# Splitting stored operands ahead of weight preparation, and a ninth early pair, in the two MLPs of a hybrid decoder trunk

## The chip, the core and the metric

The kernel runs on one core of one Trainium2 chip. The metric is device time in microseconds (us) of one execution of the whole program; the figure for a kernel is the median of its runs. All data is float32 in DRAM. The engines that matter are TensorE (PE: matmuls; PEld is its weight load), VectorE (DVE), ScalarE (ACT), GpSimd (POOL) and SyncE (SP); the last two are used here to start transfers (DMAs), each through a queue of its own.

## The reference, cut to what matters

The program computes one inference step of a two-layer decoder trunk, for a prompt of 1024 tokens and 8 single-token samples that share the weights:

```python
for l in range(DEPTH):                                    # DEPTH = 2
    h = rmsnorm(x, norm_mix[l]) * (1.0 + s1) + sh1
    out = even_mixer(h, ...) if l % 2 == 0 else mamba_mixer(h, ...)
    x = x + g1 * out
    h = rmsnorm(x, norm_mlp[l]) * (1.0 + s2) + sh2
    x = x + g2 * (jnp.square(jax.nn.relu(h @ mlp_w1[l])) @ mlp_w2[l])
```

The model width is 1024 and the inner width of the MLP 4096. The change lies in the MLP alone, that is in the last line, which is computed once in each layer. `h @ mlp_w1` is called the first projection here and the product with `mlp_w2` the second.

## The kernel before, in words

**Precision.** A float32 matmul is done as three matmuls of a reduced-precision type: each operand is split into a high part (a cast on ACT) and a low part (a subtraction on DVE), and `mm3` issues high x high (L501), high weight x low activation (L504) and low weight x high activation (L505).

**Seven products.** Each MLP projection is done by a Strassen-like scheme: instead of eight products of quarter matrices there are seven, of sums and differences of quarters, and their results are combined.

**First projections.** The 4096 inner columns are 16 pairs `p` of 2 x 128 columns. A pair has seven products `q` (1 to 7) of 24 matmuls of 128x258, so a layer has 112 products. The list `AOPS` says in which order TensorE runs them, `APREP` in which order their weights are prepared. Products 1 and 2 of a pair need only the plain input; the others need sums of input halves, which DVE and ACT make in the background (`mlp_sums`, `mlp_more_sums`) while the first products run. So the first LEAD pairs run their products 1 and 2 in front (`FRONT[0]`); they are called split pairs. A split pair's partial result (`U`) is parked in DRAM (`keep`, read back by `kept`), and its product 2 too (`B`). The last TAIL=4 pairs are split in the same way, at the end. `prep` makes the weights: a raw load on SP (`raw<-W`, 512 KB, two buffers), then, for products of sums, DVE additions (L411, L412, L420), the cast on ACT (`whi`, L441) and the subtraction on DVE (`wlo`, L442). Weights of products 1 and 2 of a split pair come from one raw load, with one cast (L435) and one subtraction (L436) of 1024 columns; the other products of a pair need both of its raw loads.

**Second projections.** 64 units run in seven stages `i`: units 0 to 47 have 48 matmuls of 128x258 each, eight units a stage, and units 48 to 63 have 24. A unit needs a weight (three buffers `whi`/`wlo`) and an operand `R[i,q]` of activations, four operands a stage, in two halves each. The operands lie in DRAM (`td`), are loaded through POOL by `load_op` (`rr<-td`, two transfers of 258 KB an operand) some units ahead, and are split by `split_op`, half by half: cast on ACT (L855), subtraction on DVE (L856). In stages 2 to 5 (the third to the sixth) a weight is a sum or a difference: a second load, `t<-W` or `t<-sd`, on SP, goes into one of four buffers `t6`, then DVE adds or subtracts (L461, L465 or L463) before the cast (L466) and the subtraction (L467). Plain weights have L476 and L477. In stages 2 and 3 the sums are stored to DRAM (`sd`) and read back in stages 3 and 5. When a unit pair is finished, its result leaves PSUM (four buffers `pd`) by DVE (L985, L992); TensorE can't start the next one before a buffer is free.

Each unit's Python code ran, in this order: matmuls and evictions, `prepare` (weights for three units ahead), `split_op`, `load_op`, and background steps (`ada_steps` adds four wide matmuls, L323, at every fourth unit of layer 0). A scheduler turns the program into one order for each engine, and an engine then runs its list strictly in that order, waiting at each instruction for what it needs. The order in which the code calls `prepare` and `split_op` sets where the two stand in the lists of ACT and DVE.

Of the kernel before, what the change touches and what calls it, by code (L numbers as in the profile page):

```python
# [33 lines left out]
AHEAD = 3  # L34
# [31 lines left out]
def odd_order():  # L66
# [5 lines left out]
    for i in range(8):  # L72
        if i == 3:
            o += z(3) + out(2) + [("dt", 0)] + bcx(4)
        else:
# [5 lines left out]

HX = TT // 2
NPAIR = NFF // 2
LEAD, TAIL = 8, 4
PROD = (1, 6, 7, 5, 2, 4, 3)

ENDS = range(LEAD), range(NPAIR - TAIL, NPAIR)
# [1 line left out]
FRONT = [[(p, q) for p in r for q in (1, 2)] for r in ENDS]  # L89
BACK = lambda r, qs=PROD: [(p, q) for p in r for q in qs if p not in SPLIT or q not in (1, 2)]  # L90
AREST = (BACK(range(2, NPAIR - TAIL)) + FRONT[1] + BACK(range(NPAIR - TAIL, NPAIR - 1))
         + BACK((NPAIR - 1,), (6, 7, 4, 5, 3)))
AOPS = FRONT[0] + BACK((0, 1), (6, 7)) + BACK((0, 1), (5, 4, 3)) + AREST

APREP = (FRONT[0] + BACK((0,), (6, 7, 4, 3)) + BACK((1,), (6, 7)) + BACK((0, 1), (5,)) + BACK((1,), (4, 3)) + AREST)
APOS = {o: i for i, o in enumerate(APREP)}


# [66 lines left out]
def kernel(ctx: ExitStack, tc: tile.TileContext, A: dict):  # L165
# [220 lines left out]
    wpos = [0]  # L386
# [36 lines left out]
    def prep(kind, idx, raw=None, into=None):  # L423
# [7 lines left out]
        if kind[0] == "a":  # L431
            l, ops = int(kind[1]), APREP[2 * idx:2 * idx + 2]
            if ops in ([(p, 1), (p, 2)] for p in SPLIT):
# [49 lines left out]
    def prepare(i):  # L483
        while len(units) <= min(i, limit[0] - 1):
            units.append(prep(*order[len(units)]))
# [310 lines left out]
    def mlp(l, gi, finish, more=None):  # L796
# [47 lines left out]
        def load_op(i, q):  # L844

            pool, tag = ((big, M["tags"][0]), (ph.pool, "hr"), (big, M["tags"][1]))[BSET[i][q // 2]]
            t = pool.tile([P, KT * 520], F32R, name="rr", tag=tag, bufs=2)
            hi, lo = R[i, q] = [t[:, j * 4 * HX:(j + 1) * 4 * HX].rearrange("p (k t) -> p k t", t=HX)
                                for j in range(2)]
            d = td[BOPND[BPROD[i]]][q // 2][:, q % 2 * 4:q % 2 * 4 + 4]  # L850

            def parts():
                for c in range(0, 4, 2):
                    src = lo[:, c:c + 2].bitcast(F32)
                    tc.keep_in_program_order(S.copy(hi[:, c:c + 2], src))  # L855
                    V.tensor_sub(lo[:, c:c + 2], src, hi[:, c:c + 2].bitcast(F32))  # L856
                    yield
            for c in range(0, 4, 2):
                dma_aux(lo[:, c:c + 2].bitcast(F32), d[:, c:c + 2])
            todo.append(parts())  # L860
# [15 lines left out]
        got = []  # L876
        for i, (p, q) in enumerate(AOPS):
            n = APOS[p, q]
            while len(got) <= n // 2:
                got.append(need(f"a{l}", len(got), AHEAD - 1))  # L880
            if i == 0:
                bg.drain(hgen.pop(3, None))
                sg = bg.add(mlp_sums())
                bg.step(sg)
            elif i == 2 * LEAD:
                bg.drain(hgen.pop(2), sg)
                sg = bg.add(mlp_more_sums())
            elif i == 2 * LEAD + 4:
                bg.drain(sg)
            if i == 2 * LEAD - 4:  # L890
                kept(0)
                kept(1)
            if q == 6:
                kept(p)
                if p and p + 1 in keep:
                    kept(p + 1)
            if p in SPLIT and q == (5 if p < 2 else 6) and p != NPAIR - TAIL:
                dma_aux(slot(p, 1), B[p])
            elif (p, q) == (NPAIR - 1, 1):
                kept(NPAIR - TAIL)  # L900
                kept(NPAIR - TAIL + 1)
                dma_aux(slot(NPAIR - TAIL, 1), B[NPAIR - TAIL])
            w = 512 * (n % 2), got[n // 2]
            pt = pd()
            product(w, q, pt)
            pv = pt[:, :, 0:HX // 2]
            if q == 1:
                U[p, 1] = t2(HX)
                S.copy(v2(U[p, 1]), pv)
                if p in SPLIT:  # L910
                    keep[p] = dr.tile([P, HX], F32, name="kept", tag=f"kept{p}")
                    dma_aux(keep[p], U[p, 1])
            elif q == 6:
                U[p, 1], U[p, 2] = saved.pop(p, U[p, 1]), t2(HX)
                V.tensor_sub(v2(U[p, 2]), v2(U[p, 1]), pv)
            elif q == 7:
                U[p, 3] = t2(HX)
                V.tensor_add(v2(U[p, 3]), pv, v2(U[p, 2]))
            elif q == 5:
                c = t2(HX)  # L920
                V.tensor_add(v2(c), pv, v2(U[p, 3]))
                V.tensor_add(v2(U[p, 2]), pv, v2(U[p, 2]))
                ff_out(p, q, c, -1.0)
            elif q == 2:
                c = t2(HX) if p in SPLIT else U[p, 1]
                V.tensor_add(v2(c), pv, v2(U[p, 1]))
                ff_out(p, q, c, 1.0)
            elif q == 4:
                c = U[p, 3] if p < NPAIR - 1 else t2(HX)
                V.tensor_add(v2(c), pv, v2(U[p, 3]))  # L930
                ff_out(p, q, c, -1.0)
            else:
                V.tensor_add(v2(U[p, 2]), pv, v2(U[p, 2]))
                ff_out(p, q, U[p, 2], 1.0)
            if n % 2:
                prepare(wpos[0] - 1 + AHEAD)
            if (p, q) == FRONT[1][-1]:
                load_op(0, 0)
                load_op(0, 1)
            elif p == NPAIR - 2 and q in (7, 5, 4, 3):  # L940
                split_op()
            if (p, q) == (NPAIR - 1, 5):
                split_op(4)
                load_op(0, 2)
                load_op(0, 3)
            bg.tick(2)
# [11 lines left out]
        for n, (i, hb, q, mp) in enumerate(BOPS):  # L958
            j = n % 8
            hi, lo = need(f"b{l}", n, AHEAD - 1)  # L960
            if n == 0 and more:
                ada[0] = more()
            elif i == 6 and hb == 0 and j == 0:
                ada_steps(99)
            elif n % 4 == 0:
                ada_steps(1)
            rh, rl = R[i, q]
            seq = BSEQ if i else BFIRST
            qs = [qq for qq, mm in seq if mm == mp]
            for m in (2 * mp, 2 * mp + 1):  # L970
                if q == qs[0]:
                    pts[m] = pd()
                pt = pts[m]
                for b in range(2) if hb is None else (hb,):
                    c = slice(b * hw, b * hw + hw)
                    mm3(pt[:, b, 0:hw], [(hi[:, o:o + P], lo[:, o:o + P], rh[:, k, c], rl[:, k, c])
                                         for k, o in ((k, 256 * k + m % 2 * P) for k in range(4))],
                        q == qs[0], q == qs[-1])
                if q == qs[-1]:
                    for o, th in BOUT[BPROD[i]]:  # L980
                        mt = 4 * o + m
                        gate = mod[:, gi + mt, 0:1]
                        if hb is None:
                            xv = v2(x[:, mt, th * HX:th * HX + HX])
                            V.scalar_tensor_tensor(xv, pt[:, :, 0:hw], gate, xv, op0=ALU.mult, op1=ALU.add)  # L985
                        else:
                            xv = x[:, mt, th * HX + hb * hw:th * HX + hb * hw + hw]
                            V.scalar_tensor_tensor(xv, pt[:, hb, 0:hw], gate, xv, op0=ALU.mult, op1=ALU.add)
                        if hb != 1:
                            sv = pt[:, 0, 0:4] if th else pt[:, 1, hw - 4:hw]  # L990
                            av = acc[:, mt, 4 * th:4 * th + 4]
                            V.tensor_add(av, sv, av)  # L992
            prepare(wpos[0] - 1 + AHEAD)

            split_op(((0, 2, 1, 1, 1, 1, 1, 1), (2, 2, 1, 1, 1, 1, 0, 2), (1, 1, 0, 0, 0, 0, 0, 0))[2 if i == 6 else i][j]
                     if i in (0, 1, 6) else (1, 1, 1, 1, 1, 1, 0, 2)[j])
            at = (4, 5, 6, 7) if i else (2, 3, 6, 7)
            if j in at and i < 6 and i + 1 + at.index(j) // 2 < 7:
                load_op(i + 1 + at.index(j) // 2, (2, 3, 0, 1)[at.index(j)])

            if i == 6 and j == 7 and hb == 0:
                V.tensor_mul(acc, acc, mod[:, gi:gi + KT, 1:9])
                for k in FOURS:
                    V.tensor_add(x[:, k, 512:520], acc[:, k], xs[:, k])
            if i >= 5:
                next(fin, None)
            bg.tick()
# [1147 lines left out]
```

## Time and profile before

| | |
|---|---|
| median of 3 runs | 2747.32 us (2745.33 to 2750.24) |
| the profiled execution | 2746.34 us; its span, first to last instruction, 2744.5 us |
| TensorE busy | 2643.4 us, 96% of the span |
| DVE, ACT, POOL busy | 1981.1 us (72%), 1484.1 us (54%), 266.2 us (10%) |
| mean granted TensorE clock | 0.985 of full speed |
| layer 0: first projections, second projections | 564 to 900 us, 900 to 1258 us |
| layer 1: first projections, second projections | 2058 to 2388 us, 2388 to 2733 us |

The profile gives busy time as a sum over the span; a share near 100% for TensorE says that most of what can be won is in the few places where it stands still. Those are found in the views of waits and of time lines, where each row has a start in us from the beginning of the span, a duration, the engine, the line, the operation, output and input, and in brackets how long the engine had been idle before and which instruction or transfer released it. A matmul of 128x258 has a duration of 0.28 us, but they overlap: starts are 0.12 us apart at full clock.

### The profile page before, as it was taken

The numbers are of one execution on the slowest core, as the hardware profiler recorded it, in microseconds if no ns is written. First come the engines' busy times: TensorE is split into PE (matmuls) and PEld (weight loads), VectorE is DVE, ScalarE is ACT, GpSimd is POOL, SyncE is SP. The second block draws the span as 40 slices with busy tenths as digits, with TensorE's granted clock in tenths as the row PEclk, the third lists the DMA queues.
The fourth block names the chain that finished last, engine by engine and source line by source line (L and its number), as shares of the span: only waits on it lengthen the run. The fifth ranks groups of instructions, "written<-read, shape, count | busy, mean of one in ns | idle before, by whom it ended". The sixth has DMA issues, their size and how long they took to land. (4 is left out here: it accounts for less than half of the span.)

```text
span 2744.5 us, 49358 instructions
## 1 busy us (share of the span) xinstructions
PE 2643.4 (96%) x19450; PEld 2436.2 (89%) x19450; DVE 1981.1 (72%) x3668; ACT 1484.1 (54%) x2411; POOL 266.2 (10%) x492
## 2 busy tenths in 40 slices
PE   6999999999999999899999999999999999999898
PEld 4888877889999999899899997787779999999897
DVE  5766542588867576676999988998778776766777
ACT  5785511174455332346887777878756445433234
POOL 0000000012313200000000000000001322310000
PEclk8999999999999999999999999999999999999999
DMA  8232356446648989744554535533335655879765
GB/s 307 66 100 84 97 190 206 139 153 198 228 155 261 387 296 353 255 142 128 161 159 156 185 125 158 146 129 108 120 115 163 228 186 188 290 282 368 269 216 162
DMA packets 191064, 525.63 MB, mean 192 GB/s; under 512 B 24432, under 2 KB 42544, under 8 KB 190832
## 3 DMA queue, kind: packets, MB, share of 16 engines
q1 hardware_dynamic: 142448, 355.25, 40.5%
q0 software_dynamic: 48384, 167.23, 16.6%
q8 instruction: 153, 2.51, 0.4%
q14 instruction: 79, 0.65, 0.1%
HBM read 408.59 MB, written 113.80 MB: 190 GB/s over the span
## 5 line engine op out<-in xcount | busy, mean ns | idle before, releaser
L501 PE MATMUL pg<-hh,whi 128*128 128x256 f32 (+2 forms) x1616 | 534.8, 331 | 7.5 <-ACT hh L603 5.9
L504 PE MATMUL pd<-rr,whi 128*128 128x258 f32 x1792 | 514.9, 287 | 17.2 <-DVE rr L856 17.1
L504 PE MATMUL pg<-hl,whi 128*128 128x256 f32 (+2 forms) x1616 | 522.0, 323 | 1.9 <-DVE hl L604 1.9
L505 PE MATMUL pg<-hh,wlo 128*128 128x256 f32 (+2 forms) x1616 | 521.3, 323 | 0.0
L501 PE MATMUL pd<-rr,whi 128*128 128x258 f32 x1792 | 511.3, 285 | 3.3 <-DVE racc L992 3.3
L505 PE MATMUL pd<-rr,wlo 128*128 128x258 f32 x1792 | 510.1, 285 | 3.6 <-DVE wlo L477 2.9
L476 ACT CAST whi<-raw 128x1024 fp32r<-128x1024 f32 x222 | 231.5, 1044 | 363.0 <-PE pg L504 217.4
L477 DVE TENSOR_TENSOR wlo<-raw,whi 128x1024 fp32r<-128x1024 f32 x222 | 270.8, 1221 | 204.5 <-ACT whi L476 196.9
L504 PEld LDWEIGHTS pd<-rr,whi 128*128 128x128 f32 x1792 | 343.4, 192 | 19.3 <-DVE rr L856 18.8
L501 PEld LDWEIGHTS pd<-rr,whi 128*128 128x128 f32 x1792 | 345.1, 193 | 10.7 <-issue 10.4
L501 PEld LDWEIGHTS pg<-hh,whi 128*128 128x128 f32 x1616 | 306.7, 190 | 50.2 <-issue 17.8
L505 PEld LDWEIGHTS pd<-rr,wlo 128*128 128x128 f32 x1792 | 343.9, 192 | 4.9 <-DVE wlo L477 3.7
L504 PEld LDWEIGHTS pg<-hl,whi 128*128 128x128 f32 x1616 | 306.9, 190 | 30.2 <-issue 4.8
L505 PEld LDWEIGHTS pg<-hh,wlo 128*128 128x128 f32 x1616 | 306.4, 190 | 24.1 <-issue 0.4
L501 PE MATMUL pd<-hh,whi 128*128 128x258 f32 x1024 | 291.8, 285 | 8.1 <-ACT hh L705 4.4
L504 PE MATMUL pd<-hh,whi 128*128 128x258 f32 x1024 | 290.6, 284 | 0.8 <-DVE hh L706 0.8
L505 PE MATMUL pd<-hh,wlo 128*128 128x258 f32 x1024 | 289.2, 283 | 0.0
L466 ACT CAST whi<-t 128x1024 fp32r<-128x1024 f32 x64 | 67.1, 1048 | 253.6 <-PE pd L504 166.6
L501 PEld LDWEIGHTS pd<-hh,whi 128*128 128x128 f32 x1024 | 194.6, 190 | 10.7 <-ACT hh L705 5.1
L504 PEld LDWEIGHTS pd<-hh,whi 128*128 128x128 f32 x1024 | 194.2, 190 | 1.9 <-DVE hh L706 1.4
L505 PEld LDWEIGHTS pd<-hh,wlo 128*128 128x128 f32 x1024 | 194.5, 190 | 0.0
L501 PE MATMUL pg<-ffh,whi 128*128 128x264 f32 (+2 forms) x544 | 177.3, 326 | 0.0
(338 smaller groups left out, 5815.1 us busy)
## 6 DMA issues: line engine op xcount, KB each, us to landing
raw<-W SPq DMA_DIRECT2D x375, 512.0 KB, 4.2
td<-x POOLq DMA_DIRECT2D x224, 258.0 KB, 4.0
rr<-td POOLq DMA_DIRECT2D x112, 516.0 KB, 7.2
t<-ada SPq DMA_DIRECT2D x192, 256.0 KB, 5.4
t<-W SPq DMA_DIRECT2D x32, 512.0 KB, 5.6
sd<-t SPq DMA_DIRECT2D x32, 512.0 KB, 6.2
t<-sd SPq DMA_DIRECT2D x32, 512.0 KB, 5.7
t<-csd SPq DMA_DIRECT2D x64, 256.0 KB, 4.5
```

Source lines behind the costliest of these rows:

```text
L466: S.copy(hi, h)
L476: S.copy(hi, raw)
L477: V.tensor_sub(lo, raw, hi.bitcast(F32))
L501: mm = PE.matmul(pt, wh, xh, start=first and i == 0, stop=False)
L504: PE.matmul(pt, wh, xl, start=False, stop=False)
L505: PE.matmul(pt, wl, xh, start=False, stop=last and i == n - 1)
```

## The change

It has two parts.

1. In the first projections LEAD goes from 8 to 9: pair 8 becomes a ninth split pair. Its products 1 and 2 do not stand behind those of pair 7 but between products 6 and 7 of pair 0 and products 6 and 7 of pair 1 (`AOPS`), and their weights are prepared behind those of pair 0 (`APREP`). The conditions on `i` that were multiples of LEAD are rewritten so that the first two still hold at positions 16 and 12; the third moves from 20 to 22, which in both lists is the start of product 5 of pair 0. In each layer there is one more raw load, and 258 KB more go to DRAM and back for each of `keep` and `B`.
2. In the second projections the call of `prepare` moves from ahead of `split_op` and `load_op` to behind them.

```diff
-LEAD, TAIL = 8, 4
+LEAD, TAIL = 9, 4
 PROD = (1, 6, 7, 5, 2, 4, 3)
...
-AOPS = FRONT[0] + BACK((0, 1), (6, 7)) + BACK((0, 1), (5, 4, 3)) + AREST
-
-APREP = (FRONT[0] + BACK((0,), (6, 7, 4, 3)) + BACK((1,), (6, 7)) + BACK((0, 1), (5,)) + BACK((1,), (4, 3)) + AREST)
+AOPS = FRONT[0][:-2] + BACK((0,), (6, 7)) + FRONT[0][-2:] + BACK((1,), (6, 7)) + BACK((0, 1), (5, 4, 3)) + AREST
+
+APREP = (FRONT[0][:-2] + BACK((0,), (6, 7, 4, 3)) + FRONT[0][-2:] + BACK((1,), (6, 7)) + BACK((0, 1), (5,))
+         + BACK((1,), (4, 3)) + AREST)
...
-            elif i == 2 * LEAD:
+            elif i == 2 * LEAD - 2:
                 bg.drain(hgen.pop(2), sg)
                 sg = bg.add(mlp_more_sums())
             elif i == 2 * LEAD + 4:
                 bg.drain(sg)
-            if i == 2 * LEAD - 4:
+            if i == 2 * LEAD - 6:
                 kept(0)
                 kept(1)
...
-            prepare(wpos[0] - 1 + AHEAD)
 
             split_op(((0, 2, 1, 1, 1, 1, 1, 1), (2, 2, 1, 1, 1, 1, 0, 2), (1, 1, 0, 0, 0, 0, 0, 0))[2 if i == 6 else i][j]
                      if i in (0, 1, 6) else (1, 1, 1, 1, 1, 1, 0, 2)[j])
             at = (4, 5, 6, 7) if i else (2, 3, 6, 7)
             if j in at and i < 6 and i + 1 + at.index(j) // 2 < 7:
                 load_op(i + 1 + at.index(j) // 2, (2, 3, 0, 1)[at.index(j)])
+            prepare(wpos[0] - 1 + AHEAD)
```

Lines of the changed kernel behind the lists are one higher than before (its L857 is L856 of before). Where the instructions stand now is seen best on DVE, at three places.

The first is layer 0's second projections, around unit 27. Before (the numbers behind names tell buffers apart: `rr_10635` is the third operand of stage 3 and `rr_10699` its fourth, which unit 27 uses; `t6_10902`, `t6_10963` and `t6_11024` carry the weight sums of units 27, 28 and 29):

```order
L467 TENSOR_TENSOR wlo_10821<-t6_10823,whi_10820 128x1024
L856 TENSOR_TENSOR rr_10635<-rr_10635 128x1032 x2
L465 TENSOR_TENSOR t6_10902<-t6_10902,raw_10904 128x1024
L465 TENSOR_TENSOR t6_10963<-t6_10963,raw_10965 128x1024
L467 TENSOR_TENSOR wlo_10900<-t6_10902,whi_10899 128x1024
L856 TENSOR_TENSOR rr_10699<-rr_10699 128x1032
L465 TENSOR_TENSOR t6_11024<-t6_11024,raw_11026 128x1024
L467 TENSOR_TENSOR wlo_10961<-t6_10963,whi_10960 128x1024
L856 TENSOR_TENSOR rr_10699<-rr_10699 128x1032
```

The same place in the changed kernel (`rr_10696` is the fourth operand; `t6_10912`, `t6_10973`, `t6_11034` are the sums of units 27, 28, 29):

```order
L468 TENSOR_TENSOR wlo_10836<-t6_10838,whi_10835 128x1024
L857 TENSOR_TENSOR rr_10696<-rr_10696 128x1032
L466 TENSOR_TENSOR t6_10912<-t6_10912,raw_10914 128x1024
L466 TENSOR_TENSOR t6_10973<-t6_10973,raw_10975 128x1024
L468 TENSOR_TENSOR wlo_10910<-t6_10912,whi_10909 128x1024
L857 TENSOR_TENSOR rr_10696<-rr_10696 128x1032
L466 TENSOR_TENSOR t6_11034<-t6_11034,raw_11036 128x1024
L468 TENSOR_TENSOR wlo_10971<-t6_10973,whi_10970 128x1024
```

The second half of unit 27's operand now stands ahead of the sum of unit 29 and the low part of unit 28, and the first half ahead of the sums of units 27 and 28.

The second place is layer 1's second projections, around unit 26. Before (`rr_27146` is the operand of unit 26; `t6_27402`, `t6_27463`, `t6_27524` are the sums of units 27, 28, 29; L985 evicts the results of units 22 and 23):

```order
L465 TENSOR_TENSOR t6_27402<-t6_27402,raw_27404 128x1024
L467 TENSOR_TENSOR wlo_27262<-t6_27264,whi_27261 128x1024
L465 TENSOR_TENSOR t6_27463<-t6_27463,raw_27465 128x1024
L985 SCALAR_TENSOR_TENSOR x_25826<-pd_27083,mod_84,x_25826 128x516
...
L985 SCALAR_TENSOR_TENSOR x_25827<-pd_27108,mod_84,x_25827 128x516
L992 TENSOR_TENSOR racc_25842<-pd_27108,racc_25842 128x4
L467 TENSOR_TENSOR wlo_27332<-t6_27334,whi_27331 128x1024
L856 TENSOR_TENSOR rr_27146<-rr_27146 128x1032 x2
```

The same place in the changed kernel (`rr_27151` is the operand of unit 26; `t6_27420` is the sum of unit 27 and `t6_27481` that of unit 28):

```order
L466 TENSOR_TENSOR t6_27420<-t6_27420,raw_27422 128x1024
L468 TENSOR_TENSOR wlo_27281<-t6_27283,whi_27280 128x1024
L857 TENSOR_TENSOR rr_27151<-rr_27151 128x1032
L986 SCALAR_TENSOR_TENSOR x_25842<-pd_27099,mod_84,x_25842 128x516
...
L857 TENSOR_TENSOR rr_27151<-rr_27151 128x1032
...
L468 TENSOR_TENSOR wlo_27355<-t6_27357,whi_27354 128x1024
L857 TENSOR_TENSOR rr_27215<-rr_27215 128x1032
L466 TENSOR_TENSOR t6_27481<-t6_27481,raw_27483 128x1024
```

Both halves of unit 26's operand and its weight's low part now stand ahead of the sum of unit 28.

The third place is layer 0's first projections, behind product 6 of pair 0. Before (`raw_5869` and `raw_5871` are the two raw loads of pair 1; L915 and L918 evict products 6 and 7 of pair 0):

```order
L915 TENSOR_TENSOR t2_5907<-t6_5737,pd_5882 128x516
L411 TENSOR_TENSOR t6_5873<-raw_5871 128x512
L420 TENSOR_TENSOR t6_5878<-raw_5869,raw_5871 128x512
L412 TENSOR_TENSOR t6_5873<-t6_5873,raw_5869 128x512
L706 TENSOR_TENSOR hr_5265<-x_83,hr_5264 128x2x516
L442 TENSOR_TENSOR wlo_5868<-t6_5873,whi_5867 128x512
```

The same place in the changed kernel (`raw_5869` is now the one raw load of pair 8 and `raw_5941` and `raw_5939` are those of pair 1):

```order
L916 TENSOR_TENSOR t2_5898<-t6_5737,pd_5873 128x516
L437 TENSOR_TENSOR wlo_5868<-raw_5869,whi_5867 128x1024
L707 TENSOR_TENSOR hr_5265<-x_83,hr_5264 128x2x516
L919 TENSOR_TENSOR t2_5935<-pd_5910,t2_5898 128x516
...
L412 TENSOR_TENSOR t6_5943<-raw_5941 128x512
L421 TENSOR_TENSOR t6_5948<-raw_5939,raw_5941 128x512
L413 TENSOR_TENSOR t6_5943<-t6_5943,raw_5939 128x512
```

The weights of pair 8, which need one load and no addition, stand where those of pair 1 stood, and those of pair 1 come two evictions later.

## Rows read from the trace of the kernel before

**Rows 1.** What TensorE waited for in the second projections: total us, times, longest; the first two rows are of 900 to 1258 us (layer 0), the last of 2388 to 2733 us (layer 1).

```profile
PE pd L504 <- DVE rr L856: 7.3, 3, 3.8
PE pd L501 <- DVE racc L992: 3.3, 1, 3.3
PE pd L504 <- DVE rr L856: 9.8, 4, 4.6
```

**Rows 2.** Busy time in stretches: us, PE (count of matmuls), PEld, DVE, ACT, POOL, granted clock, share of the DMA engines, GB/s. The first seven run from the last matmul at full clock before a wait to the first one at full clock behind it; two of the matmuls counted in each had started before the stretch. The last three are other stretches of the second projections, one of layer 0 and two of layer 1.

```profile
623.41:632.47 9.06, 4.50 (x22) 4.29 (x21) 7.15 (x12) 3.03 (x5) 0.54 (x1) 0.62 0.15 60
1063.39:1072.92 9.53, 6.55 (x32) 6.34 (x31) 7.31 (x8) 2.00 (x2) 0.00 (x0) 0.64 1.00 344
1117.80:1127.41 9.61, 5.79 (x28) 5.59 (x27) 5.64 (x5) 1.41 (x2) 0.00 (x0) 0.64 0.38 127
1156.76:1164.93 8.17, 4.86 (x28) 4.68 (x27) 7.54 (x13) 4.12 (x6) 0.00 (x0) 0.79 0.63 231
2110.61:2117.33 6.72, 5.04 (x27) 4.63 (x26) 6.63 (x12) 3.34 (x6) 1.08 (x2) 0.75 0.47 121
2538.16:2547.44 9.28, 4.64 (x23) 4.43 (x22) 9.28 (x14) 2.00 (x2) 0.00 (x0) 0.63 0.65 233
2599.79:2608.81 9.02, 4.77 (x27) 4.57 (x26) 4.82 (x5) 1.42 (x2) 0.00 (x0) 0.81 0.51 175
...
1000.00:1100.00 100.00, 97.02 (x778) 92.91 (x778) 67.24 (x82) 30.27 (x31) 8.26 (x16) 0.97 0.96 354
...
2480.00:2580.00 100.00, 95.22 (x774) 94.61 (x772) 71.57 (x92) 32.41 (x33) 8.42 (x17) 0.97 0.91 340
...
2515.00:2530.00 15.00, 15.00 (x127) 15.00 (x126) 6.06 (x6) 5.91 (x6) 3.16 (x6) 1.00 1.01 410
```

**Rows 3.** The time line of DVE before unit 27 of layer 0.

```profile
1061.10 1.23 DVE L856 TENSOR_TENSOR rr<-rr 128x1032 fp32r<-128x1032 f32 x1
1063.10 1.23 DVE L465 TENSOR_TENSOR t<-t,raw 128x1024 f32<-128x1024 f32 x1 [0.78 <-issue]
1064.24 1.22 DVE L467 TENSOR_TENSOR wlo<-t,whi 128x1024 fp32r<-128x1024 f32 x1
1065.38 1.23 DVE L856 TENSOR_TENSOR rr<-rr 128x1032 fp32r<-128x1032 f32 x1
```

**Rows 4.** The two loads of that operand, in the view of one tile from 1033 to 1036 us: the issues, and the time from issue to landing.

```profile
L230 POOL DMA_DIRECT2D rr<-td x2: 528/528/528, 1033.1 to 1033.7; - x2
...
DMA to landing us min/median/max: 7.0/8.3/9.6
```

**Rows 5.** The time line of DVE before unit 26 of layer 1.

```profile
2530.13 1.22 DVE L465 TENSOR_TENSOR t<-t,raw 128x1024 f32<-128x1024 f32 x1 [3.96 <-DMA raw<-W]
...
2536.60 1.23 DVE L465 TENSOR_TENSOR t<-t,raw 128x1024 f32<-128x1024 f32 x1 [4.11 <-DMA raw<-W]
...
2541.80 2.37 DVE L856 TENSOR_TENSOR rr<-rr 128x1032 fp32r<-128x1032 f32 x2
```

**Rows 6.** The time line of DVE before unit 35, in layer 0 and in layer 1.

```profile
1118.35 1.23 DVE L465 TENSOR_TENSOR t<-t,raw 128x1024 f32<-128x1024 f32 x1 [3.62 <-DMA t<-W]
...
1120.62 1.23 DVE L856 TENSOR_TENSOR rr<-rr 128x1032 fp32r<-128x1032 f32 x1
...
2600.78 1.23 DVE L465 TENSOR_TENSOR t<-t,raw 128x1024 f32<-128x1024 f32 x1 [2.20 <-DMA t<-W]
...
2603.05 1.23 DVE L856 TENSOR_TENSOR rr<-rr 128x1032 fp32r<-128x1032 f32 x1
```

**Rows 7.** Layer 0, units 40 and 41: two issues on SP's queue, then DVE.

```profile
1138.74 0.33 SPq L224 DMA_DIRECT2D t<-sd  x1
...
1148.59 0.33 SPq L224 DMA_DIRECT2D t<-sd  x1
...
1146.20 1.22 DVE L463 TENSOR_TENSOR t<-raw,t 128x1024 f32<-128x1024 f32 x1 [5.01 <-DMA t<-sd]
...
1156.39 1.22 DVE L463 TENSOR_TENSOR t<-raw,t 128x1024 f32<-128x1024 f32 x1 [6.69 <-DMA t<-sd]
1157.53 1.22 DVE L467 TENSOR_TENSOR wlo<-t,whi 128x1024 fp32r<-128x1024 f32 x1
1158.67 0.75 DVE L985 SCALAR_TENSOR_TENSOR x<-pd,mod,x 128x516 f32<-128x516 f32 x1
```

**Rows 8.** Layer 0, the first operand of stage 1: the cast of its first half on ACT and the weight cast behind it, the time from issue to landing of its two loads (issued from 926.5 us), and the first matmul of unit 7.

```profile
938.80 1.05 ACT L855 CAST rr<-rr 128x1032 fp32r<-128x1032 f32 x1 [6.64 <-DMA rr<-td]
939.76 1.04 ACT L476 CAST whi<-raw 128x1024 fp32r<-128x1024 f32 x1
...
DMA to landing us min/median/max: 12.2/12.9/13.6
...
940.75 0.28 PE L501 MATMUL pd<-rr,whi 128*128 128x258 f32 x1
```

**Rows 9.** Layer 0, first projections, from product 7 of pair 0 to product 6 of pair 1: the two raw loads of pair 1 on SP's queue, their time to landing, and the casts on ACT and the matmul on PE that followed.

```profile
619.09 0.93 SPq L224 DMA_DIRECT2D raw<-W  x2
...
DMA to landing us min/median/max: 5.3/5.6/5.9
...
627.04 2.21 ACT L441 CAST whi<-t 128x512 fp32r<-128x512 f32 x4 [2.80 <-DVE t L420]
...
628.26 0.58 PE L501 MATMUL pd<-hr,whi 128*128 128x258 f32 x1 [4.56 <-ACT whi L441]
```

## The prediction

> **What bounds the kernel now.** TensorE does nearly all the time, so I looked for the places where it stands still. First the view of what it waited for in the two layers' second projections [rows 1]: besides one wait of 3.3 us on an eviction, the large ones are all on L856, the low part of an operand. The list of DVE shows why such an operand is late. In layer 0 its two loads landed at the latest 9.6 us after an issue at 1033.7 us, at 1043.3 us [rows 4], but its second half was split only at 1065.38 us, behind a weight sum of unit 29 and a low part of unit 28, which nobody needed yet [rows 3]. In layer 1 the two halves for unit 26 were split at 2541.80 us, behind a sum that had stood 4.11 us waiting for its raw load [rows 5]. Unit 35 shows the same in both layers, behind a sum that waited 3.62 and 2.20 us for its second load [rows 6]. So the operands are there; they stand in the queue behind weights.
>
> Second, the price. Each stretch of [rows 2] runs from the last matmul at full clock to the next one, so it holds the wait and the slow matmuls behind it. Its loss is its length less 0.12 us for each matmul that starts in it (the count less two):
>
> - layer 0: 9.53 - 30 x 0.12 = 5.93 us (unit 27); 9.61 - 26 x 0.12 = 6.49 us (unit 35); 8.17 - 26 x 0.12 = 5.05 us (unit 40, the wait on the eviction)
> - layer 1: 9.28 - 21 x 0.12 = 6.76 us (unit 26); 9.02 - 25 x 0.12 = 6.02 us (unit 35)
> - first projections: 9.06 - 20 x 0.12 = 6.66 us in layer 0 and 6.72 - 25 x 0.12 = 3.72 us in layer 1, both at product 6 of pair 1, whose raw loads could only be issued when pair 0 had given its buffers back [rows 9]
>
> Together 40.6 us. A part of each is clock: the granted clock of these stretches is 0.62 to 0.81 [rows 2], so matmuls start 0.21 us apart for a while after the wait, at the lower of the clock's two levels (1.2 GHz), where 0.12 us is the upper one (2.4 GHz). A wait that goes takes this with it.
>
> **Part 2, operands ahead of weights.** It removes and adds no instruction; it moves each cast L855 and subtraction L856 one or two places forward.
>
> *The four operand waits.* At unit 27 of layer 0 the second half takes the place that the first one had, 1061.10 to 1062.33 us [rows 3]; TensorE stopped at 1063.4. The whole 5.93 us go. At unit 35 DVE stood idle for 3.62 and 2.20 us ahead of the sum, so from 1114.73 and 2598.58 us [rows 6]; a split there ends at 1115.96 and 2599.81, and TensorE stopped at 1117.80 and 2599.79. All of 6.49 and 6.02 us go, within 0.1. At unit 26 of layer 1 both halves now stand between the sums of 2530.13 and 2536.60 us, in idle time [rows 5]: 6.76 us go. Sum 25.20 us. A few waits below 1 us with the same cause are the rest of [rows 1]; I count 1.0 us.
>
> *What is late next.* (a) Weights now stand behind operands. The sums of units 27 and 28 in layer 1 started 6.47 us apart [rows 5], held by raw loads, while a unit takes 48 x 0.12 = 5.76 us. The low part for unit 27 stands behind the sum of unit 29 too: 2536.60 + 6.47 + 1.2 + 1.2 = 2545.5 us, with the unit due at 2538.2 + 5.76 = 2543.9 and its first low-weight matmul at 2544.2. I take 1.3 us of loss (bounds 0 and 2.5).
>
> (b) In layer 0 the first operand of stage 1 lands 12.2 us after its issue, its cast runs at 938.80 and a weight cast at 939.76 [rows 8]. Unit 7's weight used to be ready before; now its cast is this second one, and its low part follows the operand's (1.15 us each) until about 942.2 us, where unit 7, begun at 940.75, needs it at 941.0. Loss 1.3 us (bounds 0.5 and 3.5, the second if the second half's landing, at 13.6 us, held a weight too).
>
> (c) Stage 5. A load t<-sd is issued when a low part has freed its buffer, the sum waits for it, and the next low part stands behind the sum: issues at 1138.74 and 1148.59, sums at 1146.20 and 1156.39 [rows 7]. One such round takes about 10 us where a unit takes 5.76, so it loses 4.1 us. The new list keeps the two rounds of layer 0, and the evictions that end the 5.05 us wait stay behind the second. TensorE comes there 12.4 us earlier, and most of the chain too, since its weights are released by TensorE's own progress. By the new order I reckon a wait of about 7.6 us instead of 5.05: 2.5 us of loss (bounds 0 and 7.5). In layer 1 the weights had some units of lead there; as TensorE gains 12.8 us, this lead is used up and one round shows: 3.5 us of loss (bounds 0 and 8.2, which is two rounds).
>
> Part 2 gives 25.2 + 1.0 - 1.3 - 1.3 - 2.5 - 3.5 = 17.6 us.
>
> **Part 1, the ninth pair.** It moves 48 matmuls, 5.76 us, into the place of the wait; they are taken out further back. In layer 0 pair 8's raw load takes the issue at 619.09 us, lands 5.3 us later at 624.4 [rows 9], and needs one cast of about 1.05 us and no addition: product (8,1) starts at 625.5, not at 628.26 us. Its low part comes 1.2 us later and costs some 1 us. Then the price: pair 1's second raw load waits for a buffer until this low part is done, about 626.8. With 5.3 us more it lands at 632.1; three additions and a cast (2.4 us) make (1,6) start at 634.5. Before, it would have had 628.26 + 5.76 = 634.0 us for the same work. So 0.5 us lost, and as much won because the standstill is in two pieces and fewer matmuls are slow: 0 (bounds -3 and +3, half the wait either way). In layer 1 the loss was smaller, 3.72 us, so the load lands near to its need and the casts without additions hide most of it: I take 2.0 us of gain (bounds 0 and 3.72). The raw load (512 KB) and four POOL transfers more in each layer lie in stretches where the DMA engines were used for 0.15 and 0.47 of the time [rows 2], so they cost nothing; in a full stretch 1.5 MB at 410 GB/s [rows 2] would be 3.7 us in each layer.
>
> **Sum.** 17.6 + 2.0 = 19.6 us. The profiled execution took 2746.34 us, so 2726.7; the median before is 1 us higher, so I forecast 2727.7 us.
>
> **A rule against it.** The stretch from 1000 to 1100 us moved 354 GB/s with the DMA engines at 0.96, that from 2480 to 2580 us 340 GB/s at 0.91; but from 2515 to 2530 us 410 GB/s passed, at 1.01 [rows 2]. The Trainium skill ("DMA: Bandwidth & Descriptors", section "Where 436 GB/s comes from") says that for transfers between HBM and SBUF the HBM side binds at about 358 GB/s. By that rule, the first stretch could shrink by 1.1 us only and the second by 5.0. The trace does not agree: its 410 GB/s lies above.
>
> **Rivals.**
> - *All waits go, and nothing new comes.* If the chain of stage 5 runs ahead with TensorE and the first projections lose their 10.4 us too, 35 to 40 us go: about 2710 us. For it: the operands land 20 us early [rows 3, 4]. Against: the rounds of [rows 7] are set by transfers. Chance 0.12.
> - *Transfers set the pace.* By the share of the DMA engines, the 100 us of the first full stretch can shrink by 4 us, not 5.93, the second is free; at a limit of 358 GB/s, by 1.1 and 5.0 of 5.93 and 6.76: 6.6 us fewer, 2734 us. Chance 0.13.
> - *The weights become the bound.* All bounds of (a) to (c) at their bad end: 26.2 - 2.5 - 3.5 - 7.5 - 8.2 = 4.5 us of gain, less up to 3 in part 1: 2742 to 2746 us, no difference that can be measured. For it: DVE's order decides, and the weights now stand last. Chance 0.14.
> - *Slower: stage 5 turns into one chain.* If not one or two but most of its eight units in each layer run a full round, ten of sixteen lose 41 us: 2747.3 - 25.6 + 41 = 2763 us (25.6 is the sum without the terms of (c)). It decides from 31 / 4.1, about eight rounds, on. Against: in the new list only two low parts of layer 0's stage 5 stand right behind the next sum. Chance 0.06.
>
> **Numbers.** My forecast has 0.55. A change of 0.2%, 5.5 us, is about what a measurement of this kernel can tell from none. Faster: 0.55 + 0.12 + 0.13 and a little of the third rival, 0.81; same 0.12; slower 0.07. Range 2711 to 2743 us: it takes in the first rival almost whole, the second, and the better end of the third.
>
> **What would show it.** In the new profile, L856 should be gone as TensorE's releaser at units 26, 27 and 35; a short wait on a low part at unit 7 of layer 0; a longer wait at unit 40 of layer 0, and one on low parts in units 38 to 41 of layer 1; in the first projections two short waits, before (8,1) and before (1,6), in place of one. I am wrong if waits on whi or wlo of the sums in stages 3 and 4 add up to more than 5 us in a layer, or if the waits in stage 5 exceed 15 us.

## The result and the profile after

The changed kernel takes 2728.93 us (median of 4 runs, 2725.7 to 2730.87), beside 2748.56 us for the kernel before: a ratio of 0.9929, 95% interval 0.9914 to 0.9944. In two later comparisons, both on one chip, it was 0.9934 (0.9911 to 0.9957) and 0.9941 (0.9923 to 0.9959). The forecast was 2727.7 us, so a gain of 19.6 us where 19.6 us (medians) and 20.6 us (spans, 2744.5 to 2723.9) were measured. The sum was right; several of its terms were not, and the two parts share the gain otherwise than forecast: in the stretches below part 2's places gave 14.7 us for 17.6, part 1's 6.7 us for 2.0. That these errors nearly cancel, so that the sum comes out to the microsecond, is luck.

The four MLP stretches, layer 0 first and second projections, then layer 1, in the view of stretches (start and end, length, busy time and count of PE, PEld, DVE, ACT, POOL, granted clock, DMA share, GB/s). Before:

```profile
564.24:900.44 336.20, 329.09 (x2691) 326.93 (x2691) 258.83 (x390) 177.68 (x288) 87.56 (x162) 0.98 0.63 209
900.44:1257.88 357.44, 343.86 (x2776) 333.85 (x2774) 238.32 (x314) 134.53 (x154) 35.29 (x67) 0.98 0.76 275
2058.01:2387.75 329.74, 326.12 (x2690) 324.40 (x2691) 245.80 (x370) 166.23 (x268) 85.95 (x159) 0.99 0.62 207
2387.75:2733.03 345.28, 333.06 (x2710) 330.40 (x2708) 237.04 (x317) 130.82 (x155) 34.76 (x66) 0.98 0.74 266
```

After:

```profile
563.11:898.33 335.22, 329.79 (x2691) 327.01 (x2691) 258.44 (x389) 177.32 (x287) 89.72 (x165) 0.98 0.64 215
898.33:1247.07 348.74, 339.15 (x2776) 328.70 (x2774) 238.07 (x313) 135.48 (x154) 35.28 (x67) 1.00 0.78 282
2049.09:2373.16 324.07, 323.70 (x2691) 322.65 (x2691) 245.58 (x369) 166.18 (x267) 87.54 (x162) 1.00 0.65 215
2373.16:2712.42 339.26, 331.10 (x2710) 329.17 (x2708) 235.98 (x317) 130.11 (x155) 35.28 (x67) 0.98 0.76 271
```

The counts of matmuls are the same; the lengths are 1.0, 8.7, 5.7 and 6.0 us less, 21.4 us in all. (The rest of the program, which the change doesn't touch, is 0.8 us longer: 2744.5 - 1368.66 = 1375.8 and 2723.9 - 1347.29 = 1376.6 us.) What TensorE waits for in the second projections, layer 0 and then layer 1, to be read beside [rows 1] (total us, times, longest):

```profile
PE pd L502 <- DVE racc L993: 7.9, 5, 4.3
PE pd L506 <- DVE wlo L478: 1.5, 2, 1.2
...
PE pd L506 <- DVE wlo L468: 6.0, 3, 3.5
...
```

No wait on an operand (L857 now) is left in either layer (the two rows left out are not of the units). In its place stand mainly evictions in layer 0 and low parts of weights in layer 1. The two large ones, with the clock that follows them, as in [rows 2] (layer 0's unit 40, layer 1's unit 33):

```profile
1146.61:1154.07 7.46, 3.21 (x16) 3.03 (x15) 7.46 (x13) 3.29 (x5) 0.00 (x0) 0.77 0.69 248
2564.69:2574.00 9.31, 5.83 (x28) 5.62 (x27) 7.95 (x16) 1.97 (x2) 0.00 (x0) 0.63 0.37 117
```

They lose 7.46 - 14 x 0.12 = 5.8 us and 9.31 - 26 x 0.12 = 6.2 us. The first is the wait of 5.05 us of before; the second is new. On DVE, from its time line, unit 33 looks so, with the issue on SP's queue behind it:

```profile
2556.54 1.23 DVE L466 TENSOR_TENSOR t<-t,raw 128x1024 f32<-128x1024 f32 x1 [4.69 <-DMA t<-W]
2557.69 1.22 DVE L468 TENSOR_TENSOR wlo<-t,whi 128x1024 fp32r<-128x1024 f32 x1
2566.05 1.23 DVE L466 TENSOR_TENSOR t<-t,raw 128x1024 f32<-128x1024 f32 x1 [7.14 <-DMA t<-W]
2567.20 1.22 DVE L468 TENSOR_TENSOR wlo<-t,whi 128x1024 fp32r<-128x1024 f32 x1
...
2558.94 0.33 SPq L225 DMA_DIRECT2D t<-W  x1
```

The low part ends at 2558.91, its buffer is free, the load is issued at 2558.94, the next sum runs at 2566.05 and the next low part, unit 33's, behind it. That is the round of [rows 7], 9.5 us long, but in stage 4 and with a t<-W.

### The profile page after: what moved, and what is told of

Its sections match the earlier page's. It is cut to its first block, busy times and chain, and to the rows that moved or that the text cites. A ratio compares the mean times of both kernels' runs of the same rounds, so it can differ in the third digit from the quotient of the medians.

```text
span 2723.9 us, 49354 instructions
## 1 busy us (share of the span) xinstructions
PE 2635.4 (97%) x19450; PEld 2428.2 (89%) x19450; DVE 1979.9 (73%) x3666; ACT 1484.3 (54%) x2409; POOL 270.5 (10%) x500
## 3 DMA queue, kind: packets, MB, share of 16 engines
q1 hardware_dynamic: 142736, 356.29, 40.6%
```

## The experiments

Twelve runs on two chips (the first four on one, the others on the second), each compared with the kernel before on its own chip by ratio. Single profiled executions differ by some us in stretches that no edit touches (the middle of the program, between the two MLPs, took 799 to 810 us), so a stage's length is used only for what repeats.

**Part 2 alone.** Against the changed kernel, with `APREP` and the conditions on `i` as before too:

```diff
-LEAD, TAIL = 9, 4
+LEAD, TAIL = 8, 4
...
+AOPS = FRONT[0] + BACK((0, 1), (6, 7)) + BACK((0, 1), (5, 4, 3)) + AREST
```

> Part 2 alone (LEAD 8 and the old order of the first projections; prepare behind split_op and load_op). Theory: the two parts act on different places and add up; from the two traces part 2 is worth 8.7 us in layer 0's second projections (357.4 to 348.7 us) and 6.0 us in layer 1's (345.3 to 339.3 us), so about 2734 us (2731 to 2737), with the first projections as before (336.2 and 329.7 us). Rival: the parts need each other, because the first projections shift when the second ones' transfers run; then 2740 us or more with second projections above 352 and 342 us, or else nearly all of the gain here, 2730 us or less.

Measured: 0.9953 (0.9936 to 0.9970), 13 us of 2748. First projections 337.0 and 329.4 us, second 350.6 and 333.9 us (6.9 and 11.4 us less than before). This profile is of the fastest of its ten executions, 2734.02 us beside a median of 2746.46 us, so the ratio is the better measure.

**Part 1 alone.**

```diff
+            prepare(wpos[0] - 1 + AHEAD)
+
             split_op(((0, 2, 1, 1, 1, 1, 1, 1), (2, 2, 1, 1, 1, 1, 0, 2), (1, 1, 0, 0, 0, 0, 0, 0))[2 if i == 6 else i][j]
...
-            prepare(wpos[0] - 1 + AHEAD)
```

> Part 1 alone (ninth pair between pairs 0 and 1; prepare ahead of split_op as before). Theory from the traces: 1.0 us in layer 0's first projections and 5.7 us in layer 1's, second projections as before (357.4 and 345.3 us): about 2742 us (2739 to 2745). Rival, the size forecast: 0 and 2 us, so 2746.5 us; the other 3.7 us of layer 1 would then be chance of the one profiled execution (short waits of 0.3 to 0.9 us at (3,4), (5,4), (7,4) that come and go).

Measured: 0.9985 (0.9969 to 1.0001), 4 us. Its stretches, first projections of layer 0 and 1:

```profile
570.18:905.43 335.25, 328.20 (x2691) 325.27 (x2691) 257.75 (x389) 176.08 (x286) 89.74 (x165) 0.99 0.64 213
...
2073.17:2398.80 325.63, 323.96 (x2690) 322.71 (x2691) 245.42 (x369) 166.05 (x267) 88.00 (x163) 1.00 0.64 215
```

They are 0.9 and 4.1 us below before, near those of the changed kernel (335.2 and 324.1 us), while its second projections wait on operands as before (7.6 us and 8.2 us of waits). So the parts act apart: 0.47% and 0.15% make 0.62%, beside 0.59 to 0.71% for both. The interval of part 1 alone just takes in 1; that it wins anything rests on the first projections of layer 1, which took 323.5 to 326.2 us in every profile with nine pairs and 329.4 and 329.7 us in the two with eight.

**The ninth pair in front, not between.**

```diff
-AOPS = FRONT[0][:-2] + BACK((0,), (6, 7)) + FRONT[0][-2:] + BACK((1,), (6, 7)) + BACK((0, 1), (5, 4, 3)) + AREST
+AOPS = FRONT[0] + BACK((0, 1), (6, 7)) + BACK((0, 1), (5, 4, 3)) + AREST
```

(and `APREP` in the same way)

> Both parts, but the ninth pair's products 1 and 2 stand with those of the other eight in front of pair 0, not between pairs 0 and 1. Theory: its worth is that it covers the time in which pair 1's raw loads land, so the wait of some 4.5 us before (1,6) in layer 0 and of 1 to 3 us in layer 1 comes back: about 5 to 8 us slower than the changed kernel, 2734 to 2737 us. Rival: one more early pair helps wherever it stands (it gives the background sums more time): 2729 us, no wait at (1,6) above 2 us.

Measured: 0.9922 (0.9897 to 0.9947), not slower than the changed kernel. My theory of the placement fell, though the wait came back where I said. The waits of TensorE in its layer 0 first projections, and of the changed kernel's:

```profile
PE pd L502 <- ACT hh L706: 4.4, 1, 4.4
PE pd L502 <- ACT whi L442: 3.9, 1, 3.9
PE pd L505 <- DVE hh L707: 0.8, 2, 0.5
...
```

```profile
PE pd L502 <- ACT hh L706: 4.4, 1, 4.4
PE pd L502 <- ACT whi L442: 2.3, 3, 1.4
PE pd L505 <- DVE hh L707: 1.0, 2, 0.6
PE pd L502 <- DVE t L919: 0.7, 1, 0.7
PE pd L506 <- DVE wlo L443: 0.6, 1, 0.6
...
PE pd L506 <- DVE wlo L437: 0.2, 1, 0.2
```

With all nine pairs in front there is one wait of 3.9 us at (1,6), as before the change; placed between, it is three shorter ones on whi, the first already at product 6 of pair 0, which comes 5.76 us sooner than with nine in front, and some on other things. The length is 334.8 us here and 335.2 us there: the place moves the waiting and does not shorten it. In layer 1 the stretch takes 323.5 us with nine in front and 324.1 us with the ninth between, so its gain comes with the ninth pair and not with the pair's place. In time the rival held; its sign, no wait above 2 us at (1,6), did not.

**Sums and low parts in program order on DVE.** Both parts, and:

(`op` is the sum)

```diff
...
+                tc.keep_in_program_order(op)
                 S.copy(hi, h)
-                V.tensor_sub(lo, h, hi.bitcast(F32))
+                tc.keep_in_program_order(V.tensor_sub(lo, h, hi.bitcast(F32)))
```

> The changed kernel with the sum and the low part of each second-projection weight kept in program order on DVE, so that no later sum stands ahead of an earlier low part. Theory: the waits left in the second projections (5.9 us at unit 40 of layer 0; 7.3 us at units 32 and 33 and 1.7 us at unit 40 of layer 1) are rounds low part, buffer free, load, later sum, next low part; without them about 13 us go: 2716 us (2713 to 2721). Rival: the transfers set the pace there (units need their loads later than they can land): the same waits stay, now on L467's input from ACT or the sum's load, and the time is 2726 us or more.

Measured: 0.9936 (0.9915 to 0.9958), as the changed kernel. The theory was half right. In layer 0 the wait at unit 40 was gone (stage 5 took 46.2 us, its matmuls' own time), but evictions came late at units 24 and 32 (8.0 and 6.8 us), behind later units' weights. In layer 1 the rival held: stage 4 (units 32 to 39) took 55.4 us, where the changed kernel's first profile has 53.6 us and its matmuls alone take 46.1 us, and its largest wait, 3.2 us at unit 34, was now on the cast behind a sum. So a low part behind a later sum is shown to make the wait at unit 40 of layer 0, and not those of stage 4 in layer 1.

**Evictions in program order too.**

```diff
-                            V.scalar_tensor_tensor(xv, pt[:, :, 0:hw], gate, xv, op0=ALU.mult, op1=ALU.add)
+                            ev = V.scalar_tensor_tensor(xv, pt[:, :, 0:hw], gate, xv, op0=ALU.mult, op1=ALU.add)
+                            tc.keep_in_program_order(ev)
```

> As the run with sums and low parts in program order, and the evictions of whole units (L985 of before) kept in that order too, so that an eviction never stands behind a later unit's weight. In that earlier run the waits in layer 0 had gone from unit 40 (stage 5 took 46.2 us, its matmuls' own time) to evictions at units 24 and 32 (8.0 and 6.8 us). Theory: evictions behind weights are what was left; these 15 us go and the time is some 10 us below the changed kernel. Rival: sums are late because their loads are (stores of sums hold the t6 buffers until they land, and the loads come behind them); then the wait moves to low parts at units 24 to 34 and the time stays within 5 us of the changed kernel.

Measured: 0.9916 (0.9895 to 0.9937); beside the changed kernel's 0.9934 on the same chip, no difference that can be told. Here the rival held in time and in its cause, late loads; in layer 0 the waits stayed on evictions, though (8.8 us lost at unit 24, 3.6 us at unit 32). SP's queue before unit 24 of layer 0, with the time to landing of its first store, then DVE:

```profile
1029.27 0.38 SPq L225 DMA_DIRECT2D sd<-t  x1
...
DMA to landing us min/median/max: 9.2/9.2/9.2
...
1038.55 0.33 SPq L225 DMA_DIRECT2D t<-sd  x1
1038.97 0.38 SPq L225 DMA_DIRECT2D sd<-t  x1
1039.40 0.42 SPq L225 DMA_DIRECT2D raw<-W  x1
...
1032.63 1.23 DVE L462 TENSOR_TENSOR t<-t,raw 128x1024 f32<-128x1024 f32 x1 [2.28 <-DMA t<-W]
...
1050.48 1.23 DVE L466 TENSOR_TENSOR t<-t,raw 128x1024 f32<-128x1024 f32 x1 [5.69 <-DMA raw<-W]
```

The store of an earlier sum, issued at 1029.27, took 9.2 us to land; then, at 1038.55, the t<-sd for whose buffer it had stood could go, and only behind it a raw load, whose buffer the sum of 1032.63 had freed at 1033.9. The sum that needs it waited 5.69 us, until 1050.48.

**Stores one unit sooner.**

```diff
-            while sums and sums[0][0] <= idx - 2:
+            while sums and sums[0][0] <= idx - 1:
```

> The changed kernel with each sum stored to DRAM one unit sooner (so its t6 buffer comes free sooner, in stages 2 to 4). Theory: the 7.3 us at units 32 and 33 of layer 1 are a chain store landed, buffer free, t<-W, sum, low part; a store some 6 us sooner takes 5 us or more of it away: 2 to 5 us faster than the changed kernel. Rival: SP's queue then waits at the store for its sum and the raw loads behind it come later: no gain, or some us slower, with waits on raw<-W.

Measured: 0.9926 (0.9902 to 0.9951): no gain, as the rival said, but not by its cause. Units 32 to 34 of layer 1 still lost 9.5 us, and the two sums before the waits waited 4.63 and 5.75 us for t<-W, not for raw<-W. Those loads were issued as soon as a low part had ended (at 2574.94 us behind one that ended at 2573.70 + 1.22), so it was not the store that held the buffer.

**Weights late only up to stage 3.**

```diff
+            if i >= 4:
+                prepare(wpos[0] - 1 + AHEAD)
+
             split_op(((0, 2, 1, 1, 1, 1, 1, 1), (2, 2, 1, 1, 1, 1, 0, 2), (1, 1, 0, 0, 0, 0, 0, 0))[2 if i == 6 else i][j]
...
-            prepare(wpos[0] - 1 + AHEAD)
+            if i < 4:
+                prepare(wpos[0] - 1 + AHEAD)
```

> The changed kernel, but from stage 4 on weights are prepared ahead of splits again, as before. Theory: the operand wait at unit 35 comes back in both layers, about 6 us each, partly covered where units 32, 33 or 40 no longer wait (7.3 us in layer 1): 5 to 12 us slower than the changed kernel. Rival: what part 2 wins in stage 4 it pays in stages 4 and 5 (weights as the bound); then this kernel is as fast as the changed one, within 3 us.

Measured: 0.9966 (0.9950 to 0.9982), 8.8 us slower by ratio than the changed kernel beside it (6.7 us by the medians; the intervals overlap a little). The waits of its second projections, layer 0 and layer 1:

```profile
PE pd L502 <- DVE racc L993: 7.1, 4, 4.3
...
PE pd L505 <- DVE rr L857: 1.7, 1, 1.7
...
PE pd L506 <- DVE wlo L468: 4.8, 2, 3.9
PE pd L505 <- DVE rr L857: 3.9, 1, 3.9
```

One wait on an operand is back in each layer, at unit 35, with its slow matmuls 3.5 and 5.7 us. So in stage 4, too, the order of splits and weights is the cause of the operand waits. That these two are the whole difference is not shown: in layer 1 no wait is left at unit 40, where the profile of the changed kernel on this chip lost 6.8 us, and 5.1 us of what layer 0 lost more than that profile lie in the last stage. Units 32 and 33 still wait for weights; but weights are prepared three units ahead, so those were still prepared late, in stage 3, and this run does not test them.

**The changed kernel again, on that chip.**

> The changed kernel again, on the chip of the other three, so that they can be compared with it there: 0.993 of the kernel before (0.991 to 0.995), and again about 8 us in layer 0's and 6 us in layer 1's second projections less than before, with waits at unit 40 of layer 0 and at units 32 and 33 of layer 1.

Measured: 0.9934 (0.9911 to 0.9957), with losses at unit 40 of layer 0 (8.4 us), unit 33 (6.2 us) and unit 40 (6.8 us, forecast none so large) of layer 1. In this profile the second projections took 353.4 and 343.4 us, 4.0 and 1.9 us less than before, not 8 and 6. Across two profiled executions of the one program unit 40 of layer 1 lost 1.7 and 6.8 us: from the end of the low part that freed the buffer to the sum behind the load it was 7.0 us in the one and 9.3 us in the other.

**Raw load ahead of the second load, stores on POOL's queue.**

```diff
-                dma(h, a)
                 raw = load_unit(*second)
+                dma(h, a)
...
-                    sums.append((idx, sumd[n, q, mp], h))
+                    dma_aux(sumd[n, q, mp], h)
```

> The changed kernel, with the raw load of a sum issued ahead of its second load on SP's queue, and the store of a sum issued on POOL's queue as soon as the sum is made (instead of on SP's, two units later). In the last runs a t<-sd stood on SP's queue until an earlier store had landed (9.2 us after its issue), with a raw load behind it whose buffer was free. Theory: the waits left in stages 3 to 5 come from SP's queue standing still and from stores that hold buffers, so most of unit 40's and units 32 to 34's waits go: 8 us or more below the changed kernel, 0.990 of the kernel before or less. Rival: the transfers themselves are the limit there (DMA engines at 0.85 to 0.96); earlier issues land later, and the time stays within 4 us of the changed kernel (0.992 to 0.995).

Measured: 1.0001 (0.9985 to 1.0018). The whole gain is gone; neither theory had that. POOL's queue before unit 24 of layer 0, then SP's, then DVE:

```profile
1034.08 1.06 POOL L231 DMA_DIRECT2D rr<-td  x2 [8.23 <-issue]
1035.14 0.54 POOL L231 DMA_DIRECT2D sd<-t  x1
1039.84 1.05 POOL L231 DMA_DIRECT2D rr<-td  x2 [4.16 <-issue]
1040.88 0.54 POOL L231 DMA_DIRECT2D sd<-t  x1
...
1045.93 0.33 SPq L225 DMA_DIRECT2D raw<-W  x1
1046.37 0.40 SPq L225 DMA_DIRECT2D t<-sd  x1
...
1056.15 1.23 DVE L466 TENSOR_TENSOR t<-t,raw 128x1024 f32<-128x1024 f32 x1 [9.11 <-DMA t<-sd]
```

A sum waited 9.11 us for its t<-sd, with two units' evictions behind it, and TensorE waited 17.4 us on evictions in layer 0. Both halves of the edit show here. The stores stood behind operand loads, which leave 5.76 us apart, a unit's time on TensorE: the sums of these two stores had ended at 1033.84 and 1038.72, so they left 1.3 and 2.2 us late. And the t<-sd that landed late stood on SP's queue behind a raw load, which could go only at 1045.93, when the sum of 1044.68 had freed its buffer. No run made one half of the edit without the other, so which of them cost the gain is open.

**The same on top of the program order on DVE.**

> The same on top of the run with sums, low parts and evictions in program order. Theory: the waits of that run (8.8 us at unit 24 and 3.6 us at unit 32 in layer 0, 6 us at units 33 and 34 in layer 1) were on sums whose raw loads had been issued late behind other entries of SP's queue; without them 12 us or more go, 0.987 of the kernel before. Rival: limit of the transfers, within 4 us of that run (0.990 to 0.993).

Measured: 0.9899 (0.9884 to 0.9915), at the rival's better edge and short of the theory's 0.987. Again beside the changed kernel on one chip:

> The kernel with sums, low parts and evictions in program order and the stores on POOL, again, beside the changed kernel on one chip. If its 0.990 of the kernel before is its own and not that chip's, it comes out 3 per mille (8 us) below the changed kernel beside it, with stage 5 of both layers at its matmuls' own 46.2 us. If it was the chip, the two are within 1 per mille.

> The changed kernel beside it: 0.993 of the kernel before, as in its two earlier comparisons (0.9929, 0.9934), with a wait of 5 to 8 us at unit 40 of layer 0 and of 6 to 12 us in stages 4 and 5 of layer 1.

Measured: 0.9893 (0.9876 to 0.9911), 2723.72 us, beside 0.9941 (0.9923 to 0.9959), 2734.91 us. The intervals stand apart, so this kernel beats the changed kernel by 0.5% and the kernel before by 1.1%. From the run with program order alone (0.9916, 0.9895 to 0.9937) it can't be told. In the stretches its MLPs take 1342.1 us, beside 1348.7 us of the changed kernel's profile of this comparison. There unit 40 of layer 0 waited 5.8 us (8.6 us lost with the slow matmuls), as expected, and stages 4 and 5 of layer 1 lost 5.9 us, just under it. POOL's queue at the same place:

```profile
1030.86 0.53 POOL L231 DMA_DIRECT2D sd<-t  x1 [7.08 <-DVE t L462]
1031.39 1.06 POOL L231 DMA_DIRECT2D rr<-td  x2
1035.57 0.54 POOL L231 DMA_DIRECT2D sd<-t  x1 [3.11 <-DVE t L462]
```

Here the store leaves as soon as its sum is made and stands ahead of the operand loads. I read from that why the same edit pays in program order and not without it. That reading is argued from these rows; no run changed the order of POOL's queue alone. Stage 5 took its own time in layer 1 (46.1 us), but 48.0 us in layer 0, where 46.2 had been expected, and a loss of 5.9 us at unit 24 is left.

## Why the prediction was right, and where not

*The four operand waits, 25.2 us.* Right. All four are gone in the changed kernel and in part 2 alone, both units 35 come back with the old order in stages 4 and 5, and part 1 alone still waits for operands 7.6 and 8.2 us in the two layers, where the kernel before waited 7.3 and 9.8 us [rows 1]. The reading that the queue and not the transfers made operands late is shown.

*(a) Weights behind operands, 1.3 us at unit 27 of layer 1.* Wrong place and too small. Unit 27 lost nothing. Units 32 and 33 lost 1.35 and 6.2 us. The step that failed is the one that let the lead of layer 1's weights be spent in stage 5 only, at (c): TensorE gained 6.8 us at unit 26, and the rounds of stage 4 met it there at once. Before, waits for t<-W were in the list of DVE at the same place:

```profile
2576.55 1.23 DVE L465 TENSOR_TENSOR t<-t,raw 128x1024 f32<-128x1024 f32 x1 [4.77 <-DMA t<-W]
...
2583.86 1.23 DVE L465 TENSOR_TENSOR t<-t,raw 128x1024 f32<-128x1024 f32 x1 [3.80 <-DMA t<-W]
```

TensorE came too late to feel more of them than 0.6 us at unit 33. That the lead was used up is argued from these rows. Why the second of these waits then grew to 7.14 us is open, and so is what would take it away, as the run with sums and low parts in program order left the waits of stage 4.

*(b) Unit 7, 1.3 us.* 0.6 us at unit 7 and 1.6 us at unit 8, on an eviction behind the operand's splits: 2.2 us in all, inside the bounds of 0.5 and 3.5. In another profile of the same program unit 7 alone lost 3.8 us, above them.

*(c) Stage 5.* 5.05 became 5.8 us in layer 0 where I said 7.6 (without a working for it), and 1.7 us in layer 1 where I said 3.5; 8.4 and 6.8 us in another execution. In layer 0 the mechanism is the one named; that a low part behind the next sum makes it is shown by the run in program order, which takes all of layer 0's wait away, and that it does not pay by itself is shown there too.

Part 2 was to give 17.6 us and gave 14.7 in the first two profiles, and 13 us by ratio alone. More was lost at units 8, 32 and 33 and on new evictions' waits of 0.8 to 1.6 us at units 24, 28 and 32 of layer 0, which I had not counted, and less at (c).

*Part 1, 0 and 2.0 us.* The step that failed is the one that gave the ninth pair its worth by its place, over the wait for pair 1's loads: with the pair in front both layers took as long as with it between. In layer 0 the gain was 1.0 us, inside the bounds, but by waits that came sooner and were shorter. In layer 1 5.7 us, above my upper bound of 3.72. Beside the wait at (1,6), which went altogether, the short waits on whi went. The rows of waits of layer 1's first projections, before and after:

```profile
PE pd L501 <- ACT whi L441: 2.8, 4, 1.1
PE pd L501 <- ACT whi L435: 0.9, 1, 0.9
PE pd L505 <- DVE wlo L442: 0.6, 1, 0.6
...
```

```profile
PE pd L502 <- ACT whi L436: 0.9, 1, 0.9
PE pd L502 <- ACT t L814: 0.3, 1, 0.3
```

The bound took in the one stretch of [rows 2] and not the short waits behind it. Why these go with a ninth pair was not tried and stays open.

*The rivals.* That all waits go (2710 us) failed on the weights. That transfers set the pace was to cost 1.9 us by the DMA engines' share; all of units 26 and 27 was won, so it did not show. The Trainium skill ("DMA: Bandwidth & Descriptors", "Where 436 GB/s comes from") gives a limit of about 358 GB/s for HBM. The traces do not agree: 15 us of the kernel before moved 410 GB/s [rows 2], and in the fastest kernel a stretch of 56 us came out just above it, at 362 GB/s:

```profile
1044.00:1100.00 56.00, 51.84 (x416) 49.71 (x415) 37.38 (x46) 16.77 (x17) 9.42 (x18) 0.97 0.97 362
```

That the weights become the bound came true in part: the waits of 5.8, 1.35, 6.2 and 1.7 us named above are left, some 15 us of the 40.6 us that were there to win. The slower rival, stage 5 as one chain, did not come.

*The signs.* L856 is gone at units 26, 27 and 35, unit 7 waits for a low part, unit 40 of layer 0 waits longer (4.3 us for 3.3), and in layer 1 unit 40 waits for a low part. Of the two short waits in the first projections the one before (1,6) came (0.7 us); before (8,1) TensorE did not wait for whi, only 0.2 us for the low part behind it. The limits for being wrong were kept by the waits themselves and passed where the slow matmuls behind them are counted: in layer 1 units 32 and 33 waited 4.6 us in all (7.55 us with the slow matmuls) where 5 us was the limit, and in another profile the two stages 5 waited 9.5 us (15.2 us with them) where it was 15.

## What to carry to other kernels

When an operand's data is there and its consumer still waits, read the list of the engine that prepares it, and look for work needed later that stands in front and waits for something else; moving it costs nothing on the path until the work moved back has used up its lead. Price that lead before the change: the waits that a late TensorE hides now are the next ones to be seen, at the first place where TensorE gains time, not the last. In a list that is run strictly in order, look whether a sum, the low part that frees its buffer, and an eviction stand in the order in which they are needed, and whether a transfer stands behind one that waits for something else. Here neither cure paid alone: program order won nothing that could be told, and the new order of the transfers lost the whole gain; together they won 0.5%.

## What had not been expected of the hardware

The same round takes longer in one execution of a program than in another: 7.0 us in one and 9.3 us in another from a low part's end to the sum that waited for the load behind it, so that one unit lost 1.7 us and 6.8 us, with the ratio to the kernel before the same within its interval. A store of 512 KB took 9.2 us to land in a stretch where the DMA engines were used for 0.89 of the time, and a raw load of another buffer, queued behind the load that needed the store's buffer, left 5.5 us after its own was free.
